# Four of six parts of the down projection as seven block products, with two weight sums of each block formed by accumulating transfers

## The chip, the cores and the metric

The kernel runs on one core of a Trainium2 chip. The metric is the device time of one execution in microseconds (us). A time that comes from a profile is that of one profiled execution, counted from the start of its span.

## The reference, cut to what matters

Two decoder layers run over 512 tokens of width 1024, all in float32. Each ends in a gated feed-forward of width 2816, and that is where the change lies:

```python
def _swiglu(h, w_gate, w_up, w_down):
    return (jax.nn.silu(h @ w_gate) * (h @ w_up)) @ w_down

for layer in range(DEPTH):
    ...
    h = h + _swiglu(_rmsnorm(h, norm_ffn[layer]), w_gate[layer], w_up[layer], w_down[layer])
return _rmsnorm(h, norm_final)
```

Layer 0 mixes tokens by stick-breaking attention, layer 1 by dilated attention with softmax; both are left alone, apart from where two of their constants are loaded.

## The kernel before, in words

Activations lie with features on the 128 partitions and the 512 tokens along the free axis. `H` holds the residual stream (8 tiles of 128x512), `X` its normalized copy, `VO` the hidden activations of the feed-forward, `R` the norm factors. Every float32 operand is split into a high part `hi` and a rest `lo`, and a product of two operands takes three matmuls: hi·hi, hi·lo, lo·hi. `Weights.split` (L268) does it for a weight tile of 128x512: a copy on ScalarE (L306), then a subtraction on VectorE (L307). The rings of split tiles are called `whi`/`wlo` and `w2hi`/`w2lo`. Raw tiles come in by DMA issued on SP (L243) into the rings `raw` (8 buffers) and `raw2` (8, in the feed-forward alone). `Weights.get` splits up to six operands ahead of the one that TensorE takes next.

The feed-forward has 22 hidden tiles of 128. The first two are done plainly. The other twenty go in ten groups g of two tiles (`product`, L981). Gate, up, and the two halves of the tokens and of the width are treated as a 2x2 block product, done by seven products P1 to P7 instead of eight, in the order of `PRODUCTS` (L46). Each product has 24 matmuls of 128x256 and takes two weight operands. Three of the operands of a block are sums of raw blocks, made on VectorE: P6 needs `s2`, the sum of three blocks (two additions, L280 and L281), P5 takes the first of these two sums, P7 needs `s3` (one addition, L287), P4 a raw block, P3 `s4` (one more addition, L291). The results are taken out of PSUM by ScalarE copies (L1003, L1012, L1015) and VectorE additions (L1005, L1016, L1018, L1025), scaled by `R` (on GpSimd for the up half, L968), passed through Silu (L963, L1009), multiplied (L971) and split into `VO` (L974 on ScalarE, L977 on VectorE).

The down projection sums over the hidden tiles in six parts (`PARTS`, L23: one of two tiles, five of four). `down` (L1036) does one of eight output tiles of one part: 12 matmuls of 128x512 for a part of four tiles, one weight operand, and one addition into `H` (L751, in `residual`). The table `BESIDE` (L48) says after which product of which group a `down` stands; with one group beside eight `down` steps of the part before, two groups and one part make a cycle. The last part stands behind all products. In layer 1 it is done by `finish` (L1052) with weights kept in `X`.

A scheduler sets the order of the instructions on every engine; each engine then runs its own list in order.

Of the kernel before, what the change touches and what calls it, by code (L numbers as in the profile page):

```python
# [7 lines left out]
F = mybir.dt.float32  # L8
# [21 lines left out]
B_RINGS = {'z': 6, 'tf': 2, 'rp': 5, 'ah': 3, 'al': 3, 'hl': 2, 'mov': 4, 'sta': 4}  # L30
# [15 lines left out]
PRODUCTS = ("P1", "P2", "P6", "P5", "P7", "P4", "P3")  # L46

BESIDE = {1: {4: (0, 3), 5: (0, 3), 6: (0, 2)}, 3: {3: (1, 1), 4: (1, 1), 5: (1, 1), 6: (1, 1)},  # L48
# [4 lines left out]


def ffn_order():

    seq = [("gu", 0), ("gu", 1)]
    done = [0] * len(PARTS)

    def out(part, count):  # L60
        for _ in range(count):
            seq.append(("dn", part, done[part]))
            done[part] += 1

    for g in range(1, NF // 2):
        for i, p in enumerate(PRODUCTS):
# [13 lines left out]
def weight_stream():  # L80
# [4 lines left out]
    def unit(key, width):  # L85
        if key not in place:
            place[key] = len(units)
            units.append((key, width))
        return place[key]

    for layer in range(2):
# [10 lines left out]
        for step in ffn_order():  # L102
# [8 lines left out]
            else:  # L111
                for i in range(2):
                    f = 2 * step[1] + i
                    w = lambda r, c: unit(("w", layer, f, r, c), 512)
                    what = {"P1": lambda: ("raw", w(0, 0)), "P2": lambda: ("raw", w(0, 1)),
                            "P6": lambda: ("s2", w(1, 0), w(1, 1), w(0, 0)), "P5": lambda: ("s1",),
                            "P7": lambda: ("s3", w(1, 0), w(0, 0)), "P4": lambda: ("raw", w(1, 1)),
                            "P3": lambda: ("s4", w(0, 1))}[step[2]]()
                    ops.append(("pr", "ffn", (*what, i) if what[0][0] == "s" else what, None))
    return units, ops  # L120


# [1040 lines left out]
```

## Time and profile before

| what | value |
|---|---|
| median of 3 runs | 1211.24 us (1210.47 to 1214.7) |
| the profiled execution | 1206.98 us, its span 1205.1 us |
| TensorE busy | 1185.0 us of the span |
| VectorE busy | 1011.8 us |
| ScalarE busy | 698.5 us |
| GpSimd busy | 173.8 us |
| granted TensorE clock, mean | 0.997 of full speed |
| both feed-forwards | from about 240 to 600 us and from about 850 us to the end |

The chain of work that ended last is followed back from the last instruction; each of its rows is a time in which nothing else could have made the end earlier. A wait in the profile names the instruction whose end released the waiting engine. Matmuls overlap, so what one costs is the distance between starts in a row of them, not its own duration.

### The profile page before, as it was taken

The page shows a single profiled execution, that of the slowest core. Times are in us where ns is not written, and L with a number is a line of the kernel's source. Part 1 is how long each engine was busy: PE and PEld are TensorE (multiplying, and loading weights), DVE is VectorE, ACT ScalarE, POOL GpSimd, SP SyncE. Part 2 cuts the span into 40 slices and gives each one's busy share as a digit, 9 for nine tenths or more (in the row PEclk, how much of TensorE's full clock was granted, in tenths as well). Part 3 has the DMA queues.
Part 4 walks back from the last instruction along what each step waited for, and adds up shares of the span by engine and source line. Part 5 has one row for each costly group of instructions (what it writes and reads, how often), then busy time and mean ns, then how long its engine had stood idle before and what let it go on. Part 6 is the DMA issues. An engine that isn't in the chain of part 4 may idle for free.

```text
span 1205.1 us, 21100 instructions
## 1 busy us (share of the span) xinstructions
PE 1185.0 (98%) x7501; PEld 1059.8 (88%) x7501; DVE 1011.8 (84%) x1831; ACT 698.5 (58%) x1331; POOL 173.8 (14%) x237
## 2 busy tenths in 40 slices
PE   9999999999999999999999999999999999999997
PEld 7989888888999999999788889887789999999996
DVE  6799999899987878787868899788899878787865
ACT  6667676685544444454466677767755444445443
POOL 0000000001100000014235443110111000000111
PEclk9999999999999999999999999999999999999998
DMA  7654644234243323332154656551343333333112
GB/s 265 177 147 113 159 114 124 62 105 140 88 125 95 115 88 114 98 106 88 36 142 132 158 136 178 133 149 53 96 141 124 113 100 102 98 113 89 45 61 70
DMA packets 74360, 138.30 MB, mean 115 GB/s; under 512 B 9616, under 2 KB 13712, under 8 KB 74256
## 3 DMA queue, kind: packets, MB, share of 16 engines
q1 hardware_dynamic: 74256, 136.97, 40.0%
q8 instruction: 59, 0.97, 0.3%
q14 instruction: 45, 0.37, 0.1%
HBM read 106.00 MB, written 2.10 MB: 90 GB/s over the span
## 4 chain that ended last, share of the span: by engine, by line
PE 87%; DVE 6%; issue 2%; DMA 2%; ACT 2%; SPq 1%; POOL 1%; POOLq 0%; DVEq 0%
PE pj L387 39%; PE z L387 30%; PE t L387 12%; PE av L387 3%; PE t L703 3%; DVE wlo L307 1%; DMA mov<-hl 1%; DMA raw<-wflat 1%; DVE w2lo L307 0%; DVE H L751 0%; SPq L243 0%; DMA H<-xg 0%; POOL H L1076 0%; DMA rp<-rp 0%; DVE sum L281 0%
## 5 line engine op out<-in xcount | busy, mean ns | idle before, releaser
L306 ACT ACTIVATE whi<-raw 128x512 fp32r<-128x512 f32 (+1 forms) x290 | 178.7, 622 | 134.5 <-PE pj L387 52.1
L307 DVE TENSOR_TENSOR wlo<-raw,whi 128x512 fp32r<-128x512 f32 (+1 forms) x290 | 206.8, 721 | 26.0 <-ACT whi L306 23.6
L387 PE MATMUL pj<-VO,whi 128*128 128x512 f32 x568 | 180.7, 398 | 1.1 <-DVE H L751 1.0
L387 PE MATMUL pj<-X,whi 128*128 128x512 f32 x480 | 154.4, 402 | 0.4
L968 POOL TENSOR_TENSOR up<-up,R 128x512 f32<-128x512 f32 x40 | 62.4, 1563 | 490.9 <-DVE up L1016 442.6
L387 PEld LDWEIGHTS pj<-VO,whi 128*128 128x128 f32 x568 | 102.4, 189 | 23.8 <-ACT whi L306 1.1
L387 PE MATMUL pj<-VO,wlo 128*128 128x512 f32 x284 | 112.7, 397 | 0.0
L751 DVE TENSOR_TENSOR H<-H,pj 128x512 f32<-128x512 f32 (+1 forms) x120 | 79.3, 664 | 32.2 <-PE pj L387 31.5
L387 PEld LDWEIGHTS pj<-X,whi 128*128 128x128 f32 x480 | 86.9, 188 | 19.1 <-ACT X L423 0.9
L387 PE MATMUL z<-XT,whi 128*128 128x256 f32 x560 | 99.7, 280 | 0.0
L306 ACT ACTIVATE w2hi<-raw 128x512 fp32r<-128x512 f32 (+1 forms) x102 | 62.8, 617 | 59.0 <-PE z L387 17.1
L387 PE MATMUL z<-X,whi 128*128 128x256 f32 (+1 forms) x464 | 96.1, 301 | 0.0
L387 PE MATMUL pj<-X,wlo 128*128 128x512 f32 x240 | 95.2, 396 | 0.5 <-DVE wlo L307 0.5
L387 PEld LDWEIGHTS z<-XT,whi 128*128 128x128 f32 x560 | 86.2, 189 | 0.7
L387 PE MATMUL pj<-VO,w2hi 128*128 128x512 f32 x264 | 83.1, 396 | 0.4 <-ACT VO L974 0.4
L307 DVE TENSOR_TENSOR w2lo<-raw,w2hi 128x512 fp32r<-128x512 f32 (+1 forms) x102 | 71.0, 698 | 12.0 <-ACT w2hi L306 11.7
L387 PEld LDWEIGHTS z<-X,whi 128*128 128x128 f32 x464 | 74.9, 189 | 4.7
L387 PE MATMUL z<-XT,wlo 128*128 128x256 f32 x280 | 78.5, 280 | 0.0
L387 PE MATMUL pj<-whi,X 128*128 128x256 f32 x384 | 74.9, 285 | 2.1 <-DVE rp L558 2.1
L387 PE MATMUL z<-XT,w2hi 128*128 128x256 f32 x400 | 74.0, 284 | 1.7 <-ACT w2hi L306 1.0
L305 POOL TENSOR_TENSOR raw<-raw,H 128x512 f32<-128x512 f32 x48 | 58.9, 1237 | 79.0 <-DMA raw<-wflat 37.1
L387 PE MATMUL z<-X,wlo 128*128 128x256 f32 (+1 forms) x232 | 69.8, 301 | 0.0
(200 smaller groups left out, 3033.0 us busy)
## 6 DMA issues: line engine op xcount, KB each, us to landing
raw<-wflat SPq DMA_DIRECT2D x384, 256.0 KB, 2.8
mov<-hl SPq DMA_DIRECT2D x64, 256.0 KB, 4.3
sta<-hl SPq DMA_DIRECT2D x64, 128.0 KB, 2.3
rp<-rp SPq DMA_DIRECT2D x56, 64.0 KB, 2.1
raw<-wflat SPq DMA_DIRECT2D x16, 128.0 KB, 2.6
H<-xg SPq DMA_DIRECT2D x7, 256.0 KB, 5.5
outT<-H SPq DMA_DIRECT2D x2, 512.0 KB, 3.0
CS<-cs SPq DMA_DIRECT2D x1, 512.0 KB, 3.7
```

The lines of the kernel that those rows point to most:

```text
L305: nc.gpsimd.tensor_mul(v3, v3, g.unsqueeze(2).to_broadcast([128, n // m, m]))
L306: nc.scalar.activation(hi[:, :n], v, AF.Copy)
L307: nc.vector.tensor_sub(lo[:, :n], v, hi[:, :n].bitcast(F))
L387: pe.matmul(out, a, b, start=start, stop=stop, skip_group_check=True)
L703: pe.transpose(b[:, o:o + 128], pr[i][:, 128 * c:128 * c + 128], idf)
L751: dve.tensor_add(H[:, n, e], H[:, n, e], p[:, e])
L968: pool.tensor_mul(two(u), two(u), r)
```

## The change

Parts 1 to 4 of the down projection, which are four hidden tiles each, are no longer done by 8 `down` steps. Each is taken as two problems q (four output tiles each), and each problem as a 2x2 block product over two pairs of hidden tiles and two halves of the tokens, done by seven products (`down_product`, steps "dq"). One has 12 matmuls of 128x256 and one weight operand, uses the banks `pj` and `av`, and ends in one VectorE addition or subtraction into a quarter of four tiles of `H` (L1154 of the new kernel). `SPREAD` and `SPREAD_LAST` place them between the products of the next two groups. Four sums of hidden blocks, needed as moving operands, are made and split by `hidden_sums`, into slot 8 of `VO`, a new tile `GS` and a free quarter of `X`; `maskB` and `ACC` serve as scratch.

The weight sums of a block are formed in another way, for gate and up (from the second group on) and for the down blocks. The block of P7 is loaded by SP and has a second block added to it by an accumulating transfer, issued on GpSimd (`Weights.add`, L278 of the new kernel). P6 then takes one VectorE addition (L326), P5 one subtraction (L330), P7 none. After P5 a second accumulating transfer adds a block to the P6 sum, which gives the operand of P3. There are 102 such transfers of 256 KB, 52 into raw tiles and 50 into sums. `raw2` shrinks to 6 buffers. P4 of the gate and up now accumulates in the bank of P1, P6 and P7, so that the addition L1016 falls away, and the sign of the token sum it takes is turned.

To make room, `CS` is loaded at the start of the second mixer and `maskB` near the end of the first feed-forward instead of before; one ring of the second mixer (`tf`) has one buffer less.

```diff
 A_RINGS = {'z': 5, 'w': 5, 'tf': 2, 'tq': 2, 'ah': 3, 'al': 3, 'hl': 2, 'mov': 4, 'sta': 4}
-B_RINGS = {'z': 6, 'tf': 2, 'rp': 5, 'ah': 3, 'al': 3, 'hl': 2, 'mov': 4, 'sta': 4}
+B_RINGS = {'z': 6, 'tf': 1, 'rp': 5, 'ah': 3, 'al': 3, 'hl': 2, 'mov': 4, 'sta': 4}
...
 PRODUCTS = ("P1", "P2", "P6", "P5", "P7", "P4", "P3")
-BESIDE = {1: {4: (0, 3), 5: (0, 3), 6: (0, 2)}, 3: {3: (1, 1), 4: (1, 1), 5: (1, 1), 6: (1, 1)},
-          4: {0: (1, 1), 2: (1, 1), 4: (1, 1), 6: (1, 1)}, 5: {3: (2, 1), 4: (2, 1), 5: (2, 1), 6: (2, 1)},
-          6: {0: (2, 1), 2: (2, 1), 4: (2, 1), 6: (2, 1)}, 7: {3: (3, 1), 4: (3, 1), 5: (3, 1), 6: (3, 1)},
...
+BLOCKED = (1, 2, 3, 4)
+BESIDE = {1: {4: 3, 6: 2}, 2: {4: 3}}
+SPREAD = ((0, 0, 1, 1, 1, 1, 1), (2, 1, 2, 1, 2, 1, 0))
+SPREAD_LAST = ((0, 0, 1, 1, 1, 1, 1), (1, 1, 1, 1, 1, 1, 0))
 def ffn_order():
     seq = [("gu", 0), ("gu", 1)]
-    done = [0] * len(PARTS)
...
+    first = 0
...
             seq.append(("pr", g, p))
-            out(*BESIDE.get(g, {}).get(i, (0, 0)))
-    for part in range(len(PARTS)):
-        out(part, 8 - done[part])
+            for _ in range(BESIDE.get(g, {}).get(i, 0)):
+                seq.append(("dn", 0, first))
+                first += 1
+            if part in BLOCKED:
+                for _ in range(spread[i]):
+                    seq.append(blocked.pop(0))
+    assert first == 8
+    seq += blocked + [("dn", len(PARTS) - 1, n) for n in range(8)]
     return seq
...
+    def block_operand(p, block, dma, ops_of):
+        w = lambda r, c: unit(block(r, c), 512)
+        low = lambda: unit(block(1, 0), 512, block(0, 0) if dma[0] else None)
+        last = () if dma[1] else (w(0, 1),)
+        what = {"P1": lambda: ("raw", w(0, 0)), "P2": lambda: ("raw", w(0, 1)),
+                "P6": lambda: ("s2", ops_of, block(0, 1) if dma[1] else None, low(), w(1, 1),
+                               *(() if dma[0] else (w(0, 0),))),
+                "P5": lambda: ("s1", ops_of, w(0, 0)), "P7": lambda: ("raw", low()),
+                "P4": lambda: ("raw", w(1, 1)), "P3": lambda: ("s4", ops_of, *last)}[p]()
+        return what
...
+                    ops.append(("pr", "ffn", block_operand(step[2], lambda r, c: ("w", layer, f, r, c),
+                                                           (step[1] > 1,) * 2, (layer, f)), None))
+            else:
+                _, part, q, p = step
+                ops.append(("dq", "ffn", block_operand(p, lambda r, c: ("d", layer, part, q, r, c),
+                                                       (True, (part, q) != (BLOCKED[-1], 1)),
+                                                       (layer, part, q)), None))
...
+            self.uring.append("raw2" if ffn and q % 14 >= 8 else "raw")
             q = q + 1 if ffn else 0
         q = 0
...
+    RAW, RAW2 = 8, 6
     W, W2 = 4, 3
...
+    def add(self, n):
+        while self.adds and self.adds[0][0] < n:
+            _, t, key = self.adds.pop(0)
+            self.nc.gpsimd.dma_start(t, self.source(key, 512), accum_op=OP.add)
     def load(self):
         u = self.nload
...
         t = self.pools[ring].tile([128, 512], F, name=ring, bufs=self.size[ring])
-        self.nc.sync.dma_start(t[:, :n], bass.AP(
...
         self.rt[u] = t[:, :n]
+        if added:
+            self.later_add(self.first[u], t, added)
...
                 self.load()
+        self.add(u + 1)
         r = [self.rt[v] for v in self.used(self.ops[u])]
         if what[0] == "raw":
             v = r[0]
         elif what[0] == "s2":
-            s1, s2 = (self.pools["sum"].tile([128, 512], F, name="sum", bufs=4) for _ in range(2))
-            nc.vector.tensor_add(s1, r[0], r[1])
-            nc.vector.tensor_add(s2, s1, r[2])
-            self.sums[what[-1]] = (s1, s2)
-            v = s2
+            v = self.pools["sum"].tile([128, 512], F, name="sum", bufs=4)
+            if len(r) == 3:
+                nc.vector.tensor_add(r[0], r[0], r[2])
+            nc.vector.tensor_add(v, r[0], r[1])
+            self.sums[what[1]] = v
         elif what[0] == "s1":
-            v = self.sums[what[-1]][0]
-        elif what[0] == "s3":
-            nc.vector.tensor_add(r[0], r[0], r[1])
             v = r[0]
+            nc.vector.tensor_sub(v, self.sums[what[1]], v)
         else:
-            v = self.sums.pop(what[-1])[1]
-            nc.vector.tensor_add(v, v, r[0])
+            v = self.sums.pop(what[1])
+            if r:
+                nc.vector.tensor_add(v, v, r[0])
         n = v.shape[1]
         ring = self.oring[u]
         if ring == "held":
-            t = self.kept[:, self.ops[u][2][1] - self.kept0]
+            t = self.kept[:, (self.ops[u][2][1] - self.kept0 + 4) % 8]
...
         nc.scalar.activation(hi[:, :n], v, AF.Copy)
         nc.vector.tensor_sub(lo[:, :n], v, hi[:, :n].bitcast(F))
+        if what[0] == "s2" and what[2]:
...
         ahead = self.AHEAD[self.ops[u][1]]
+        self.add(u + ahead + 4)
...
     ACC = sb.tile([128, 512], F, name="ACC")
-    CS = sb.tile([128, 2, 512], F, name="CS")
...
+                dve.scalar_tensor_tensor(t[0], b21, -1.0, t[1], op0=OP.mult, op1=OP.subtract)
...
+        free = X[:, 0:4, :, 256:512].rearrange("p (s c) i n -> p s i c n", s=2)
+        two = lambda t: t.rearrange("p (f n) -> p f n", f=2)
+        sums = {"P5": [two(VO[:, 8, 512 * i:512 * i + 512]) for i in range(2)],
+                "P6": [two(GS[:, i, :]) for i in range(2)],
...
-                act.activation(hi, two(g), AF.Copy)
+                if not (upper and e == 1):
+                    act.activation(hi, two(g), AF.Copy)
             def low():
-                dve.tensor_sub(lo, two(g), hi.bitcast(F))
+                if not (upper and e == 1):
...
+                high("P7", maskB)
+                low("P6", ACC)
+            def fourth():
+                b21 = st["B21"]
+                dve.scalar_tensor_tensor(b21, b21, -1.0, ACC, op0=OP.mult, op1=OP.subtract)
+                high("P4", b21)
+            for n, f in enumerate((lambda: high("P5", ACC), second, third, fourth, lambda: low("P7", maskB),
+                                   lambda: low("P4", st["B21"]))):
+                after(5 + n, f)
         def product(g, p, XT):
-            new = {"P1": ("a", zb), "P2": ("b", tb), "P5": ("e", zb), "P4": ("c", tb)}.get(p)
+            new = {"P1": ("a", zb), "P2": ("b", tb), "P5": ("e", zb)}.get(p)
             if new:
                 st[new[0]] = new[1]()
-            name = {"P1": "a", "P6": "a", "P7": "a", "P2": "b", "P5": "e", "P3": "e", "P4": "c"}[p]
-            bank = st[name]
...
                     stepped()
-            a, b, c, e = (st.get(k) for k in "abce")
...
             elif p == "P7":
-                st["u", 0], st["u", 1] = (W.pools["w2"].tile([128, 512], F, name="up", bufs=2) for _ in range(2))
+                st["u", 1] = TS()
...
+            new = {"P1": ("da", pjbank), "P2": ("db", avbank), "P5": ("de", pjbank)}.get(p)
+            if new:
+                st[new[0]] = new[1]()
+            bank = st[{"P2": "db", "P5": "de", "P3": "de"}.get(p, "da")]
+            wh, wl = W.get("dq")
+            f = PARTS[part][0]
+            def x(k, i):
+                if p in sums:
+                    return sums[p][i][:, k, :]
+                c, e = {"P1": (0, 0), "P2": (1, 0), "P3": (1, 1)}[p]
+                return VO[:, (f + 2 * c + k) % 8, 512 * i + 256 * e:512 * i + 256 * e + 256]
+            for i in range(2):
+                out = bank[:, 256 * i:256 * i + 256]
+                for k in range(2):
+                    w = slice(256 * i + 128 * k, 256 * i + 128 * k + 128)
+                    mm(out, wh[:, w], x(k, 0), bool(new) and i == 0 and k == 0, False)
+                    mm(out, wh[:, w], x(k, 1), False, False)
+                    mm(out, wl[:, w], x(k, 0), False, k == 1)
+            for r, e, op in {"P1": [(0, 0, OP.add)], "P2": [(0, 0, OP.add)], "P6": [(0, 1, OP.add)],
+                             "P5": [(1, 1, OP.subtract)], "P7": [(1, 1, OP.subtract)],
+                             "P4": [(1, 0, OP.subtract)], "P3": [(0, 1, OP.add)]}[p]:
+                h = H[:, 4 * q + 2 * r:4 * q + 2 * r + 2, 256 * e:256 * e + 256]
+                dve.tensor_tensor(h, h, two(bank), op=op)
+            stepped()
         def down(part, n):
...
                         break
                     else:
```

On TensorE, a part of four tiles took 96 matmuls of 512 columns and now takes 168 of 256 columns; the whole list grows from 7477 matmuls to 8053.

Two other engines show how instructions move. First GpSimd, in the feed-forward of layer 0 (L968 in the old and L1026 in the new kernel is the multiply of the up half by `R`; L437 and L656 before and L305 behind belong to the stages around). Before, the feed-forward is one row of its list:

```order
L656 MEMSET w 128x2
L437 TENSOR_TENSOR ACC<-H 128x512
L866 TENSOR_TENSOR s<-s,R 128x512 x2
L968 TENSOR_TENSOR up<-up,R 128x512 x18
L305 TENSOR_TENSOR raw<-raw,H 128x512 x5
```

Now, for one cycle of two groups (L278 is the issue of an accumulating transfer into a raw tile or a sum):

```order
L1026 TENSOR_TENSOR s<-s,R 128x512 x2
L278 DMA sum<-wflat 128x512 x3
L278 DMA raw_5296<-wflat 128x512
L278 DMA raw<-wflat 128x512
L278 DMA raw_5412<-wflat 128x512
L1026 TENSOR_TENSOR s<-s,R 128x512 x2
L278 DMA sum<-wflat 128x512 x2
L278 DMA raw<-wflat 128x512
L278 DMA sum<-wflat 128x512
L278 DMA raw<-wflat 128x512
L278 DMA raw_5797<-wflat 128x512
```

Twelve issues stand between four multiplies, and each waits, at the head of the list, for the load or the VectorE instruction that its tile comes from.

Second, VectorE, in the middle of the same feed-forward, with the numbers of the buffers. Before, all additions of weight blocks are its own (L280, L281, L287, L291):

```order
L291 TENSOR_TENSOR sum_5047<-sum_5047,raw_4746 128x512
L307 TENSOR_TENSOR wlo_5086<-sum_5021,whi_5085 128x512
L280 TENSOR_TENSOR sum_5355<-raw2_4966,raw2_5125 128x512
L287 TENSOR_TENSOR raw2_4966<-raw2_4966,raw2_4885 128x512
L751 TENSOR_TENSOR H_61<-H_61,pj_5089 128x512
L307 TENSOR_TENSOR wlo_5105<-sum_5046,whi_5104 128x512
L281 TENSOR_TENSOR sum_5356<-sum_5355,raw2_4885 128x512
```

Now, where a block is formed with a transfer: the first row frees the buffer into which SP then loads `raw_5273`, GpSimd's transfer adds to it, and the last row takes the sum:

```order
L350 TENSOR_TENSOR wlo_5270<-raw_4602,whi_5269 128x512
L1100 TENSOR_TENSOR g_5211<-g_5211,t_5249 128x512
L350 TENSOR_TENSOR w2lo_5291<-raw_4621,w2hi_5290 128x512
L1101 TENSOR_TENSOR g_5211<-g_5211,R_64 128x512
L1154 TENSOR_TENSOR H_61<-H_61,pj_5288 128x2x256
L350 TENSOR_TENSOR w2lo_5314<-raw2_4833,w2hi_5313 128x512
L350 TENSOR_TENSOR w2lo_5334<-raw2_4835,w2hi_5333 128x512
L350 TENSOR_TENSOR wlo_5355<-raw2_4895,whi_5354 128x512
L326 TENSOR_TENSOR sum_5578<-raw_5273,raw_5294 128x512
```

So the load and the accumulating transfer stand beside the eight VectorE instructions ahead of the last row. Of the 26 sums of that kind in a layer, five stand eight rows behind the row that frees the buffer, two stand ten rows behind, and the other nineteen 12 to 34. A whole cycle has 93 VectorE instructions in the new list and 80 in the old.

## Rows read from the trace of the kernel before

**Rows 1.** The page: busy times, GB/s in 40 slices of the span, chain that ended last.

```profile
PE 1185.0 (98%) x7501; PEld 1059.8 (88%) x7501; DVE 1011.8 (84%) x1831; ACT 698.5 (58%) x1331; POOL 173.8 (14%) x237
...
GB/s 265 177 147 113 159 114 124 62 105 140 88 125 95 115 88 114 98 106 88 36 142 132 158 136 178 133 149 53 96 141 124 113 100 102 98 113 89 45 61 70
...
PE 87%; DVE 6%; issue 2%; DMA 2%; ACT 2%; SPq 1%; POOL 1%; POOLq 0%; DVEq 0%
```

**Rows 2.** Busy time in stretches of the first feed-forward, from its third tile on.

```profile
core 0: us, PE busy (x) PEld busy (x) DVE busy (x) ACT busy (x) POOL busy (x), PEclk, DMA share, GB/s
277.00:306.00 29.00, 28.04 (x183) 24.91 (x182) 28.53 (x49) 14.84 (x28) 3.29 (x2) 1.00 0.46 146
306.00:326.00 20.00, 20.00 (x171) 20.00 (x170) 18.87 (x30) 10.73 (x18) 3.17 (x2) 1.00 0.43 132
326.00:346.00 20.00, 19.42 (x141) 18.13 (x140) 19.43 (x32) 11.22 (x20) 0.85 (x2) 1.00 0.43 125
...
406.00:466.00 60.00, 60.00 (x423) 55.85 (x422) 48.73 (x77) 28.47 (x48) 5.81 (x4) 1.00 0.36 106
```

**Rows 3.** The chain of waits, same feed-forward: start, us, engine and tile, instructions.

```profile
421.76 2.81 PE pj L387 x12
...
517.66 5.68 PE z L387 x48
...
574.66 22.69 PE pj L387 x96
```

**Rows 4.** Timeline of VectorE, first and last of sixteen instructions without a wait between.

```profile
450.08 0.69 DVE L960 TENSOR_TENSOR s<-s,R 128x512 f32<-128x512 f32 x1
...
459.10 0.69 DVE L307 TENSOR_TENSOR wlo<-raw,whi 128x512 fp32r<-128x512 f32 x1
```

**Rows 5.** Waits of VectorE, 340 to 520 us: for whom, us in total, times, longest.

```profile
DVE H L751 <- PE pj L387: 11.3, 11, 1.5
DVE s L971 <- POOL up L968: 7.1, 6, 1.2
DVE w2lo L307 <- ACT w2hi L306: 5.8, 9, 0.7
DVE wlo L307 <- ACT whi L306: 3.1, 7, 0.7
DVE VO L977 <- ACT VO L974: 2.1, 3, 0.7
```

**Rows 6.** DMA issues: KB each, median us from issue to landing.

```profile
raw<-wflat SPq DMA_DIRECT2D x384, 256.0 KB, 2.8
mov<-hl SPq DMA_DIRECT2D x64, 256.0 KB, 4.3
...
cst<-cst SPq DMA_DIRECT2D x1, 256.0 KB, 5.5
```

**Rows 7.** The multiply that GpSimd does, and the VectorE product behind it; durations in ns, least, median, most.

```profile
L968 POOL TENSOR_TENSOR up<-up,R x40: 1287/1612/2827, 288.7 to 1157.4; 128x512 f32<-128x512 f32 x40
```

**Rows 8.** ScalarE's copy after the fifth product; durations as above.

```profile
L1015 ACT ACTIVATE up<-z x20: 579/582/587, 287.2 to 1154.1; 128x512 f32<-128x512 f32 x20
```

**Rows 9.** Timeline of TensorE, end of the first feed-forward: the last part.

```profile
574.66 0.71 PE L387 MATMUL pj<-VO,w2hi 128*128 128x512 f32 x2 [0.40 <-ACT VO L974]
```

**Rows 10.** Timeline of ScalarE, same place.

```profile
573.95 0.63 ACT L974 ACTIVATE VO<-s 128x512 fp32r<-128x512 f32 x1 [0.24 <-DVE s L971]
```

More of the change, by code (lines that the diff above doesn't have):

```diff
@@ L83, in weight_stream, with unit @@
     units, ops, place = [], [], {}
[L85 to L89, printed above, removed]
+    def unit(key, width, added=None):
+        if (key, added) not in place:
+            place[key, added] = len(units)
+            units.append((key, width, added))
+        return place[key, added]
+    def block_operand(p, block, dma, ops_of):
[8 more added lines that the diff above has]
+        return what
     for layer in range(2):
@@ L110, in weight_stream @@
                             ("raw", unit(("dn", layer, *step[1:]), 128 * (b - a))), None))
-            else:
+            elif step[0] == "pr":
                 for i in range(2):
                     f = 2 * step[1] + i
[L114 to L119, printed above, removed]
+                    ops.append(("pr", "ffn", block_operand(step[2], lambda r, c: ("w", layer, f, r, c),
[5 more added lines that the diff above has]
+                                                       (layer, part, q)), None))
     return units, ops
@@ L150, in pack_weights @@
             t = cols((w_gate, w_up)[r][l], f)[:, 512 * c:512 * c + 512]
+        elif kind == "d":
+            _, _, part, q, r, c = key
+            f = 128 * (PARTS[part][0] + 2 * c)
+            t = np.concatenate([cols(w_down[l][f:f + 256], 4 * q + 2 * r + i) for i in range(2)], axis=1)
         else:
@@ L213, in __init__ @@
                 first.setdefault(u, n)
+        self.first = first
+        self.last_sum = {op[2][1]: n for n, op in enumerate(self.ops) if op[2][0] == "s4"}
         self.uring, self.oring = [], []
@@ L263, in ready @@
             return False
-        if zone == "held" and now <= self.last_product:
+        if zone == "held" and now <= self.last_product[what[1] - self.kept0 >= 4]:
             return False
@@ L760, in whole @@
                 return fs_done[1]
+            if layer:
+                CS = CSS["CS"] = rings["pool"].tile([128, 2, 512], F, name="CS")
+                sp.dma_start(CS, cs_d.rearrange("p (a n) -> p a n", a=2))
             pair = [(tb if layer else pjbank)() for _ in range(2)]
@@ L998, in product @@
                     stepped()
-            a, b, c, e = (st.get(k) for k in "abce")
+            a, b, e = (st.get(k) for k in "abe")
             f0 = 2 * g
-            if p == "P1":
-                st["g", 0] = TS()
-                act.activation(st["g", 0], a, AF.Copy)
+            if p in ("P1", "P6"):
+                h = int(p == "P6")
+                st["g", h] = W.pools["sum"].tile([128, 512], F, name="g", bufs=4)
+                act.activation(st["g", h], a, AF.Copy)
             elif p == "P2":
@@ L1115, in ffn @@
                         down(*step[1:])
+                if layer == 0:
+                    sp.dma_start(maskB, cst_d[:, 640:1152])
                 while later:
@@ L1125, in trunk @@
     W.kept = X
-    W.kept0 = next(u for u, (key, _) in enumerate(W.units) if key[:3] == ("dn", 1, len(PARTS) - 1))
+    W.kept0 = next(u for u, (key, *_) in enumerate(W.units) if key[:3] == ("dn", 1, len(PARTS) - 1))
     for c in range(8):
```

82 lines of the change are left out of this document (56 added, 26 removed), and 2 rows, old and new, of the table BESIDE.

## The prediction

> **What bounds the kernel now.** I read the page first. TensorE is busy for 1185.0 of 1205.1 us, VectorE for 84% and ScalarE for 58%, and 87% of the chain that ended last is TensorE [rows 1]. Second, the busy times by stretch of a feed-forward [rows 2]. From 406 to 466 us TensorE is busy for 60.00 of 60, at a granted clock of 1.00, and VectorE for 48.73. Third, the chain of waits [rows 3]: there it is only TensorE, one product or `down` after another. So time falls when TensorE has fewer columns to stream, as long as VectorE, the next in line, keeps up. The same rows show where it doesn't quite: from 326 to 346 us VectorE is busy for 19.43 of 20 and TensorE for 19.42.
>
> The profiled execution took 1206.98 us, 4.3 under the median of 1211.24. I work with differences and put them on the median. Some 0.5%, 6 us, is what a measurement can tell from no change.
>
> **TensorE: what is removed and added.** A `down` of 12 matmuls of 512 columns takes 2.81 us, 0.234 us each; 48 matmuls of 256 columns take 5.68 us, 0.1183 us each [rows 3]. A part had 96 × 0.234 = 22.5 us and gets 168 × 0.1183 = 19.9 us. That is −2.6 us a part, and with four parts in two layers, eight, **−20.8 us**. A cycle (two groups of seven products of 24 matmuls, and one part) was 336 × 0.1183 + 22.5 = 62.2 us and would be 59.6.
>
> A rule speaks against this. The Trainium skill ("TensorE: Matmul & The Clock Gate", Back-to-back issue gap) puts a sustained stream with weight loads at about 81 ns per matmul of 128 columns and 131 ns at 512: short matmuls pay for their weight loads. By it, 168 × at least 81 ns is 13.6 us against 96 × 131 ns = 12.6 us, an estimate in which a part gets slower. The trace disagrees, since its 512 columns take 234 ns and its 256 columns half of that, in the stream of weight loads of this very kernel.
>
> **VectorE: instructions.** In a stretch without a wait, 15 steps take 459.10 − 450.08 = 9.02 us, 0.601 us each [rows 4]. Before, a cycle has 80 instructions: 36 splits of weights, 16 additions of blocks, 8 additions into `H`, 20 for the hidden tiles. Now it has 93: 42 splits, 12 block sums, 14 into `H`, 18 for the hidden tiles (L1016 is gone), 7 for the hidden sums. So 48.1 us of 62.2 become **55.9 us of 59.6, 93.7%**. The nearest rows are the busy stretches [rows 2]: at 94.4% (306 to 326 us) TensorE lost nothing, at 97.1% (326 to 346) it lost 0.58 us in 20, 2.9%, and at 98.4% (277 to 306) 0.96 in 29, 3.3%. By these, instructions alone cost nothing yet.
>
> VectorE also waits, and in the steady stretch mostly where it had time to: 11.3 us in 180 for TensorE at L751, which is slack and shrinks. For ScalarE it waited 5.8 + 3.1 + 2.1 = 11.0 us [rows 5], 3.8 us a cycle. At 94.4% busy such waits did no harm, so I cost them at nothing; with VectorE held elsewhere they come on top. ScalarE gets about 12 more instructions of 0.6 us a cycle and had 28.47 busy of 60: no bound.
>
> **The accumulating transfers.** None is in this trace. The nearest rows [rows 6] are a plain load of the same 256 KB at 2.8 us, a copy of 256 KB that reads and writes SBUF at 4.3 us, and the slowest 256 KB at 5.5 us. Less than 2.8 us is excluded, because the same bytes come from the same memory and one more read is added. I take 4.3, since an accumulating transfer also reads what it writes. The buffer must first be loaded, so from its release to the sum of P6 it takes 2.8 + 4.3 = 7.1 us, 11.8 VectorE rows. Nineteen of the 26 sums into raw tiles in a layer have 12 rows or more. Five have 8 (4.8 us) and are 2.3 us short; two have 10 (6.0 us) and are 1.1 short: 13.7 us, less 5.7 where two stand next to each other and wait at the same time, 8 us a layer, 2.0 a cycle. The 50 sums that lead to P3 have at least 13 rows, all in time. VectorE then needs 57.9 of 59.6 us, 97.1%, at which the row loses 2.9%. The sums stand six operands ahead of TensorE, and part of a wait is eaten by that lead: I take half, 1.45% or 0.87 us a cycle, **+6.9 us** over eight. At 2.8 us the path is 5.6 us, 9.3 rows, and the cost is near 0. At 5.5 us it is 8.3 us, 13.8 rows, and the wait some 17 us a layer (second rival).
>
> The same list of GpSimd carries the multiplies L968, of 1287 to 2827 ns [rows 7]. A transfer behind one can be issued up to 2.8 us late. With four multiplies among twelve transfers I count that within the bounds above. Traffic rises from 24 to 36 transfers of 256 KB a cycle, so the 106 GB/s of the steady stretch become about 166; the first slice of the span shows 265 [rows 1], so that room is there. SP loses nothing: its loads are as many per block, and the added ones are GpSimd's.
>
> **Smaller edits.** P4 of gate and up uses the bank of P7 and so waits for ScalarE's copy, 582 ns [rows 8]. A down product of 12 × 0.118 = 1.4 us stands between and hides it; without that cover it would cost 0.6 us in each of 20 groups, 12 us at most. At the end of a feed-forward the last product is followed by work that hides the last hidden tile. The copy into `VO` ends at 574.58 [rows 10], and TensorE waited only 0.40 us for it [rows 9], after 8.4 us of cover. Now three down products (4.3 us) and the first half of two `down` (2.8) stand there, 7.1 us: up to 1.8 us lost a layer. I take **+2 us** for both, between 0 and 3.6. `CS` and `maskB`, loaded later, and the ring `tf` of one buffer, lie in stages that VectorE and TensorE share: 0, and at most a few us if a load of `CS` is awaited.
>
> **Sum:** −20.8 + 6.9 + 2 = −11.9, so 1195.1 against 1206.98 in the profiled execution, and 1211.2 − 11.9 = **1199 us** on the median.
>
> **The rivals.** *First, the whole gain.* Transfers land within 3 us, or the lead of six operands eats every wait: −20.8 + 2, about 1192. For it: at 94.4% VectorE cost TensorE nothing. Against: it stands on a plain load's price for more than a load.
>
> *Second, slower: VectorE is held at the sums of P6.* If transfers land after 5.5 us or later, its waits are 17 us a layer, 4.3 a cycle, and the waits for ScalarE (3.8) stay whole: 55.9 + 4.3 + 3.8 = 64.0 us a cycle, 1.8 over the old 62.2. Eight cycles give +14, the tail 2: about 1227. It decides from 6.3 us of waiting a cycle (62.2 − 55.9) on. For it: GpSimd's own work varies between 1.29 and 2.83 us beside a busy VectorE [rows 7], and one such delay of 1.5 us added to 4.3 gives 5.8. The Trainium skill ("SBUF — State Buffer", A bandwidth-pool intuition that's wrong) says that a transfer issued on GpSimd, some 620 ns alone, takes some 3100 ns beside a VectorE copy, because GpSimd can't write its descriptors until VectorE releases the port that they share. No row here shows such a transfer. Against it: nineteen of 26 sums have slack to spare.
>
> *Third, nothing is left.* VectorE's waits come out near those 6.3 us a cycle, and the gain of TensorE is given back: within 6 us of 1211. It needs a transfer of about 5 us.
>
> *Fourth, weight loads bound the short matmuls.* They were busy for 55.85 of 60 us with 423 matmuls, 0.132 us each [rows 2]. Were that a floor, a part would still take 168 × 0.132 = 22.2 us, 0.3 less than before, 2 us in eight; with 6.9 + 2 the time would be about 1218. Against it: 256 columns run at 0.118 [rows 3]. This is the mechanism of the Trainium skill's issue gap above.
>
> **How the numbers follow.** The forecast, a gain of 6 to 16 us, 1195 to 1205, has 0.33: its instruction counts are firm, its transfer time is not. The first rival has 0.31, because VectorE's instructions alone fit. The second has 0.21, the third 0.14, the fourth 0.01, as [rows 3] contradict it. So faster is 0.33 + 0.31 = 0.64, same 0.14, slower 0.22. The range begins at 1189, the whole gain without a loss at the tail, and ends at 1226, short of the far half of the second rival: 0.05 below and 0.13 above are left out.
>
> **What would show it.** In the new profile, down products should run at 0.118 us a matmul, and TensorE's idle time in the steady stretches should be 0.5 to 1.5 us a cycle, released by VectorE's splits or by its additions into `H`. VectorE should be above 90% busy there, its longest waits at L326, released by transfers into raw tiles. Transfers should land in 3.5 to 5 us. If they land under 3, the first rival holds; if the idle time before L326 exceeds 6 us a cycle, the second or third. Wrong altogether would be a matmul pitch over 0.13 us, a lower granted clock, or a wait at a place not named here, such as GpSimd's multiply held up behind transfers that wait for loads.

## The result, and the profile after

The changed kernel takes **1271.23 us** (median of 4 runs, 1267.61 to 1273.11) against 1210.86 of the kernel before in the same series: a ratio of 1.0489, 95% interval 1.0456 to 1.0521. It is 60 us slower. 1199 us was forecast, and the range ended at 1226.

The page of the changed kernel has these lines on busy time, on the chain that ended last and on DMA issues (columns as in [rows 1] and [rows 6]):

```profile
PE 1187.2 (94%) x8077; PEld 1089.5 (86%) x8077; DVE 1082.7 (86%) x1925; ACT 740.0 (58%) x1423; POOL 255.2 (20%) x339
...
PE 41%; DVE 16%; DMA 10%; issue 5%; ACT 2%; POOL 1%; DVEq 0%; POOLq 0%; SPq 0%; ACTq 0%
...
raw<-wflat SPq DMA_DIRECT2D x384, 256.0 KB, 3.1
mov<-hl SPq DMA_DIRECT2D x64, 256.0 KB, 4.5
raw<-wflat POOLq DMA_DIRECT2D x52, 256.0 KB, 4.9
sum<-wflat POOLq DMA_DIRECT2D x50, 256.0 KB, 5.6
```

TensorE has 41% of the chain, DMA 10% and VectorE 16%. These shares can't be set beside the 87% of before as they stand: the new chain can be followed back only to 312 us, so they add up to about 75%. Of what it covers TensorE has a little over half. The accumulating transfers are the two rows on POOL's queue: 4.9 us into raw tiles, 5.6 into sums. The steady part of the first feed-forward, in three stretches of about one cycle each (columns as in [rows 2]):

```profile
330.00:400.00 70.00, 64.23 (x536) 63.35 (x535) 60.54 (x95) 35.24 (x62) 16.90 (x18) 1.00 0.60 136
400.00:470.00 70.00, 62.77 (x490) 61.96 (x489) 59.67 (x94) 34.62 (x61) 15.91 (x17) 0.93 0.58 136
470.00:540.00 70.00, 64.59 (x521) 63.98 (x520) 60.88 (x96) 36.29 (x64) 17.71 (x19) 0.95 0.61 138
```

TensorE, busy without a gap before, now idles 5.4 to 7.2 us in 70, and its granted clock is 0.93 and 0.95 on the mean of the last two stretches. VectorE isn't full either: 9 to 10 us of each stretch are not busy. Its waits, 340 to 520 us (for whom, us in total, times, longest), and those of TensorE:

```profile
DVE sum L326 <- DMA raw<-wflat: 19.4, 4, 8.4
DVE sum L326 <- DVE w2lo L350: 0.6, 1, 0.6
DVE sum L326 <- DVE wlo L350: 0.4, 1, 0.4
```

```profile
PE pj L433 <- DVE H L1154: 10.4, 5, 3.7
PE pj L433 <- ACT g L1021: 2.1, 2, 1.4
PE z L433 <- ACT g L1098: 1.9, 1, 1.9
```

Nearly all waiting of VectorE is at L326, the sum of P6, for a transfer into a raw tile; a fifth such wait, of 7.8 us, ends at 520.80 and is not in these rows. The waits of [rows 5], 11.3 us for TensorE and 11.0 for ScalarE, are gone: VectorE runs behind everyone, and TensorE waits for its additions into `H`. No wait of VectorE in these rows is for TensorE, so the slower clock can have cost these cycles little. That it cost nothing isn't shown, since the chain also passes through TensorE at half the clock. There 12 matmuls of 256 columns take 2.90 us, and 1.42 us a little later:

```profile
458.10 2.90 PE pj L433 x12
...
464.69 1.42 PE pj L433 x12
```

The chain shows one path through a transfer in full:

```profile
380.40 0.61 DVE wlo L350
381.01 0.02 issue
381.03 2.52 DMA raw<-wflat
383.55 0.02 issue
383.57 0.04 POOLq L278
383.62 0.49 issue
384.11 5.65 DMA raw<-wflat
389.76 0.04 DVEq L326
389.80 0.04 issue
389.84 0.09 DVE sum L326
```

The split at 380.40 frees a raw buffer. SP's load lands 2.5 us later, GpSimd needs 0.56 us to see it and issue, the accumulating transfer takes 5.65 us, and at 389.84 VectorE may add: **8.8 us**, 14.7 rows of 0.601 us, where I had taken 7.1.

A second thing shows in the lists of GpSimd and VectorE (start, duration):

```profile
391.82 2.97 POOL L1026 TENSOR_TENSOR s<-s,R 128x512 f32<-128x512 f32 x2 [6.85 <-DVE s L1107]
```

```profile
391.65 0.68 DVE L1154 TENSOR_TENSOR H<-H,pj 128x512 f32<-128x512 f32 x1
392.25 1.40 DVE L350 TENSOR_TENSOR wlo<-raw,whi 128x512 fp32r<-128x512 f32 x1
393.57 0.68 DVE L1154 TENSOR_TENSOR H<-H,pj 128x512 f32<-128x512 f32 x1
394.16 1.18 DVE L350 TENSOR_TENSOR wlo<-raw,whi 128x512 fp32r<-128x512 f32 x1
```

Beside GpSimd's two multiplies, two subtractions of VectorE on SBUF tiles take 1.40 and 1.18 us instead of 0.68, and each holds up the next. The addition between them, which reads PSUM, is not stretched.

To compare kernels I use the time of three cycles of layer 0 (from the third to the ninth Silu of the first half, L1009 before, L1103 now; layer 1 agrees within 2.4 us): 335.36 to 521.19 us is 185.8 before, 339.37 to 547.82 is 208.4 now. With 206.4 in layer 1, these six cycles hold 43 of the 60 us; the rest lies ahead of them and behind them in the feed-forwards.

### The profile page after: what moved, and what is told of

It is laid out like the page before. It is cut to its first block, busy times and chain, and to the rows that moved or that the text cites. A ratio compares the mean times of both kernels' runs of the same rounds, so it can differ in the third digit from the quotient of the medians.

```text
span 1265.8 us, 22739 instructions
## 1 busy us (share of the span) xinstructions
PE 1187.2 (94%) x8077; PEld 1089.5 (86%) x8077; DVE 1082.7 (86%) x1925; ACT 740.0 (58%) x1423; POOL 255.2 (20%) x339
## 4 chain that ended last, share of the span: by engine, by line
PE 41%; DVE 16%; DMA 10%; issue 5%; ACT 2%; POOL 1%; DVEq 0%; POOLq 0%; SPq 0%; ACTq 0%
PE pj L433 17%; PE z L433 16%; DMA raw<-wflat 9%; DVE wlo L350 5%; PE t L433 4%; DVE w2lo L350 2%; PE av L433 2%; DVE H L1154 2%; PE t L749 1%; DMA mov<-hl 1%; DVE raw L330 1%; DVE g L1034 1%; DVE g L1018 1%; DVE g L1117 1%; ACT whi L349 0%
## 5 line engine op out<-in xcount | busy, mean ns | idle before, releaser
L349 ACT ACTIVATE whi<-raw 128x512 fp32r<-128x512 f32 x331 | 201.2, 619 | 151.9 <-PE pj L433 91.4
L350 DVE TENSOR_TENSOR wlo<-raw,whi 128x512 fp32r<-128x512 f32 x331 | 241.8, 735 | 15.2 <-ACT whi L349 14.2
L433 PE MATMUL pj<-X,whi 128*128 128x512 f32 (+1 forms) x592 | 178.2, 385 | 24.8 <-DVE H L1154 13.2
L433 PE MATMUL pj<-VO,whi 128*128 128x512 f32 (+1 forms) x544 | 142.0, 350 | 15.6 <-DVE H L797 7.8
L433 PE MATMUL z<-XT,w2hi 128*128 128x256 f32 x656 | 125.0, 290 | 8.0 <-ACT g L1098 6.7
L433 PEld LDWEIGHTS z<-XT,w2hi 128*128 128x128 f32 x656 | 105.4, 197 | 10.3 <-ACT g L1098 7.8
L433 PE MATMUL pj<-X,wlo 128*128 128x512 f32 (+1 forms) x296 | 112.0, 378 | 0.2 <-DVE wlo L350 0.2
L433 PE MATMUL z<-XT,w2lo 128*128 128x256 f32 x328 | 94.4, 289 | 1.2 <-DVE w2lo L350 1.0
L278 POOL DMA_DIRECT2D raw<-wflat x52 | 45.1, 879 | 245.4 <-DMA raw<-wflat 73.7
L433 PE MATMUL pj<-VO,wlo 128*128 128x256 f32 (+1 forms) x272 | 94.2, 346 | 0.0
L1026 POOL TENSOR_TENSOR s<-s,R 128x512 f32<-128x512 f32 x40 | 58.0, 1472 | 99.1 <-DVE s L1107 70.9
L326 DVE TENSOR_TENSOR sum<-raw 128x512 f32<-128x512 f32 x36 | 29.3, 814 | 55.3 <-DMA raw<-wflat 53.8
```

Of the source, the lines that this page charges most:

```text
L278: self.nc.gpsimd.dma_start(t, self.source(key, 512), accum_op=OP.add)
L326: nc.vector.tensor_add(v, r[0], r[1])
L349: nc.scalar.activation(hi[:, :n], v, AF.Copy)
L350: nc.vector.tensor_sub(lo[:, :n], v, hi[:, :n].bitcast(F))
L433: pe.matmul(out, a, b, start=start, stop=stop, skip_group_check=True)
L1026: pool.tensor_mul(two(u), two(u), r)
```

## The experiments

The theory: VectorE is the bound, and transfers that land too late hold it at L326. Rivals: the list of VectorE alone is too long, or short matmuls and a falling clock of TensorE cost it. All ratios are to the kernel before on the same chip.

**No transfers.**

```diff
-            self.nc.gpsimd.dma_start(t, self.source(key, 512), accum_op=OP.add)
+            pass
```

> The accumulating transfers are left out, so the weight sums lack the block that each would have added; loads, VectorE's additions and all products stay, and the scheduler orders the lists anew. Theory (VectorE is held at the sums of P6 by transfers that land too late): the 68.5 us of waiting at L326 go, a cycle falls from 69 to between 59.6 and 61 us, and the time to 1192 to 1204 us, as the whole gain was forecast. First rival (VectorE's instruction list alone is the new bound, 93 rows at 0.64 us): a cycle of at least 60 us and the waits at L326 replaced by others, 1204 to 1215 us. Second rival (short matmuls or the clock of TensorE cost it): over 1230 us.

Measured: 1200.69 us, 0.9911 (0.9887 to 0.9935). Three cycles take 183.1 us, 61.0 each. Busy times from 340 to 520 us, and the only wait of VectorE:

```profile
340.00:520.00 180.00, 177.49 (x1488) 176.26 (x1488) 177.74 (x276) 103.95 (x182) 16.55 (x12) 1.00 0.36 105
```

```profile
DVE sum L326 <- DMA raw<-wflat: 1.8, 5, 0.5
```

So the transfers cost 1271.2 − 1200.7 = **70.5 us**; this includes what the new order of the lists does. In the changed kernel, the waits for transfers at L326 come to nearly as much over the whole run (us in total, times):

```profile
  DVE sum L326: 68.5, 16
```

The theory holds for them, and the time lies in its range. But what the first rival named shows in the rest: VectorE is now full (177.74 of 180), at 177.74 / 276 = 0.644 us an instruction instead of 0.601, and a cycle takes 61.0 us, not 59.6.

**Plain transfers.** Same lists, no addition in the transfer.

```diff
-            self.nc.gpsimd.dma_start(t, self.source(key, 512), accum_op=OP.add)
+            self.nc.gpsimd.dma_start(t, self.source(key, 512))
```

> The 102 transfers on GpSimd are plain loads into the same tiles instead of accumulating ones, so the sums are replaced by the second block; all lists stay the same. Theory, in the form that the read before the write makes them late: they land in 2.8 to 3.3 us instead of 4.9, the path from a freed buffer to the sum falls from 9 to about 7 us, the waits at L326 to under half of 68.5 us, and the time to 1215 to 1235 us. Rival (issue on GpSimd and its list in order make them late, the addition costs little): they land in over 4.4 us and the time stays over 1255 us.

Measured: 1230.92 us, 1.016 (1.0133 to 1.0188). The theory holds. The landing times, VectorE's largest wait from 340 to 520 us, and the waits for transfers at L326 in the whole run:

```profile
raw<-wflat POOLq DMA_DIRECT2D x52, 256.0 KB, 3.2
sum<-wflat POOLq DMA_DIRECT2D x50, 256.0 KB, 3.1
```

```profile
DVE sum L326 <- DMA raw<-wflat: 13.6, 4, 3.9
```

```profile
  DVE sum L326: 33.0, 14
```

The addition costs 1.7 us a transfer into a raw tile and 2.5 into a sum, and 40 of the 70 us. The other 30 go with the 33.0 us of waits that are left, for a second transfer behind the first: 2.8 + 0.6 + 3.2 us is still more than the 4.8 us that five of the sums of a layer have.

The median landing hides two cases. Of the 102 accumulating transfers of the changed kernel, 43 were issued with no other one under way and landed in a median of 4.2 us, 59 with another under way and landed in 5.8. Plain ones took 3.0 and 3.2 us. Of the transfers into sums 35 of 50 are of the second kind, of those into raw tiles 24 of 52. Whether one transfer holds up the other wasn't tried by itself.

**All sums on VectorE; then only those into raw tiles.**

```diff
-                                                           (step[1] > 1,) * 2, (layer, f)), None))
+                                                           (False, False), (layer, f)), None))
...
-                                                       (True, (part, q) != (BLOCKED[-1], 1)),
+                                                       (False, False),
```

In the second kernel the two new lines are:

```diff
+                                                           (False, step[1] > 1), (layer, f)), None))
...
+                                                       (False, (part, q) != (BLOCKED[-1], 1)),
```

> All weight sums on VectorE, no transfers: 12 more VectorE instructions a cycle, 105 of 0.601 to 0.641 us, 63.1 to 67.3 us a cycle against 62.2 before and 69 with the transfers. Theory (VectorE is the bound, the transfers hold it): no wait at L326, 1215 to 1250 us, faster than the change. Rival (TensorE's short matmuls or its clock cost it, VectorE has room): no better than 1262 us.

> Only the 52 transfers into raw tiles are taken back, as additions on VectorE; the 50 into P6 sums stay: 99 VectorE instructions a cycle, 59.5 to 63.5 us. Theory (it is the transfers into raw tiles, with a load before them and a full ring, that hold VectorE; those into sums have time): waits for transfers under 10 us in all and 1198 to 1228 us, the best of these versions that compute everything. Rival (any transfer in GpSimd's list holds VectorE): waits for sums appear in their place and the time is over 1245 us.

Measured: 1248.53 us, 1.0309 (1.0287 to 1.0331), and 1237.01 us, 1.0213 (1.0176 to 1.0249). The first kernel's busy times from 340 to 520 us:

```profile
340.00:520.00 180.00, 169.34 (x1393) 165.59 (x1393) 179.75 (x283) 93.45 (x164) 21.66 (x12) 1.00 0.33 100
```

Here VectorE is busy for 179.75 of 180 with no transfer and no wait: its list is the bound, 105 × 0.635 = 66.7 us a cycle, and 66.0 were measured. That the change is still 23 us slower than this says that a transfer costs VectorE more by waiting than the addition that it saves. The second kernel missed its range by 9 us: 99 rows at 0.637 make 63.1, and its waits didn't vanish (VectorE, 340 to 520 us):

```profile
DVE raw L325 <- DMA raw<-wflat: 5.7, 3, 2.4
DVE sum L326 <- DMA raw<-wflat: 1.6, 1, 1.6
```

These are for plain loads on SP. Why loads come late here and not in the kernel without any transfer wasn't tried.

**An earlier load, and the multiply on VectorE.**

```diff
-                "P2": lambda: ("raw", w(0, 1)),
+                "P2": lambda: (low(), ("raw", w(0, 1)))[1],
```

```diff
-                pool.tensor_mul(two(u), two(u), r)
+                dve.tensor_mul(two(u), two(u), r)
```

> The change, with the block of P7 (the one that a transfer adds to) loaded ahead of that of P2 instead of behind it, one or two loads earlier. Theory (the path from the freed buffer to the sum of P6, 9 us with load, issue and landing, is longer than its lead): the lead grows by one to two loads of 2.9 us each, the waits at L326 fall from 68.5 us to 20 to 45, and the time to 1225 to 1255 us. Rival (14 raw buffers that are held longer set the pace, whatever the order): within 8 us of 1271, with waits moved to other loads.

> The change, with the multiply of the up half (L1026, four a cycle) on VectorE instead of GpSimd. Theory (VectorE is the bound, and its rows beside a GpSimd multiply are stretched, by 3.5 to 4.1 us a cycle): four more rows of 0.602 us are 2.4, and 3.5 to 4 us go, so a cycle gains 1.1 to 1.6 and the time falls by 9 to 13 us, to 1258 to 1263. Rival (the stretch comes from the issue of transfers on GpSimd): the stretch stays and the time grows by some 19 us.

Measured: 1226.82 us, 1.0145 (1.012 to 1.017), 44 us better than the change, with 27.2 us of waits for transfers at L326 instead of 68.5, as the theory has it. The order of two loads gives back as much as the addition in the transfer cost, as a path too long for its lead would have it, and a ring of too few buffers would not. The multiply gives 1246.31 us, 1.03 (1.0281 to 1.0319), 25 us better where 9 to 13 were expected. Busy times and the largest wait of VectorE, 340 to 520 us, with the multiply moved:

```profile
340.00:520.00 180.00, 169.54 (x1386) 168.40 (x1385) 160.05 (x265) 93.90 (x166) 28.67 (x33) 0.97 0.63 148
```

```profile
DVE wlo L350 <- ACT whi L349: 14.6, 3, 6.7
```

160.05 / 265 = 0.604 us an instruction: the stretch is gone, so it was the multiplies' and not the transfers'. The waits for transfers at L326 are gone from this stretch too, but others took their place, at splits behind ScalarE. A cycle fell by 4.1 us, and the instructions explain 0.8 of it: 97 × 0.604 = 58.6 us instead of 93 × 0.639 = 59.4. The rest is waiting that went, which the expectation didn't have. The multiplies no longer stand between the transfers in GpSimd's list; that this is why is not shown.

**Both repairs.** Both edits above.

> The change with both repairs: the block of P7 loaded earlier and the multiply on VectorE. VectorE has 97 rows a cycle, 58.4 us without stretch, TensorE 59.6. The waits were 9.5 to 11 us a cycle, 5 to 6 with the earlier load, 6 to 8 with the multiply. Theory (the two repairs add up): 2 to 4 us of waiting are left, 60.4 to 62.4 us a cycle, 1197 to 1214 us. Rival (transfers in one list, 12 a cycle of some 5 us from issue to landing, hold VectorE whatever is done): 4 us of waiting or more, over 1214 us.

Measured: 1218.8 us, 1.0074 (1.0057 to 1.009): the rival. Waits of VectorE, then of ScalarE, 340 to 520 us:

```profile
DVE wlo L350 <- ACT whi L349: 13.0, 3, 7.0
```

```profile
ACT whi L349 <- DMA sum<-wflat: 15.7, 3, 8.0
```

ScalarE's copy of the P3 operand waits for the transfer into the sum, up to 8.0 us, and VectorE behind it. The longest of these waits, with the two rows of GpSimd's list ahead of it (start, duration, idle before):

```profile
429.26 0.86 POOL L278 DMA_DIRECT2D raw<-wflat  x1 [5.27 <-DVE w2lo L350]
429.80 1.22 POOL L278 DMA_DIRECT2D sum<-wflat  x1
437.11 0.63 ACT L349 ACTIVATE whi<-sum 128x512 fp32r<-128x512 f32 x1 [7.97 <-DMA sum<-wflat]
```

The transfer into the sum shows no wait of its own. It is issued at 429.80, right behind one into a raw tile that had waited 5.27 us for a split of VectorE, and takes 7.2 us to land. It is one of the 50 that I had costed at nothing.

**No transfers, and the multiply on VectorE.**

> The change without its transfers (the sums lack the block that each would have added) and with the multiply of the up half on VectorE: 97 VectorE rows a cycle, 58.4 us, against TensorE's 59.6. Theory (the term of TensorE was right, and VectorE alone stood in its way): TensorE is the bound again, 59.6 to 60.1 us a cycle, 1187 to 1195 us. Rival (short products lose something of their own): cycles of 60.6 us or more and no better than the 1200.7 us of the version without transfers.

Measured: 1190.24 us, 0.9837 (0.982 to 0.9853), a cycle of 59.6 us, and TensorE never waits from 340 to 520 us:

```profile
340.00:520.00 180.00, 180.00 (x1523) 180.00 (x1522) 177.97 (x295) 108.15 (x187) 0.00 (x0) 1.00 0.37 109
```

The term of TensorE was right: 504 matmuls of 256 columns at 0.1183 us are 59.6. And VectorE at 98.9% busy took nothing from it.

**Half of the block products, no transfers; then also the multiply on VectorE.** One problem of a part is done by products, the other four output tiles by `down`; both flags are (False, False) as above, the hidden quarter that `down` needs is split too, and the second kernel has the edit of the multiply.

```diff
-            blocked = [("dq", part, q, p) for q in range(2) for p in DOWN_PRODUCTS]
+            blocked = [("dq", part, 1, p) for p in DOWN_PRODUCTS] + [("dn", part, n) for n in range(4)]
...
-SPREAD = ((0, 0, 1, 1, 1, 1, 1), (2, 1, 2, 1, 2, 1, 0))
+SPREAD = ((0, 0, 1, 1, 1, 1, 1), (1, 1, 1, 1, 1, 1, 0))
...
-SPREAD_LAST = ((0, 0, 1, 1, 1, 1, 1), (1, 1, 1, 1, 1, 1, 0))
+SPREAD_LAST = ((0, 0, 1, 1, 1, 1, 1), (1, 1, 1, 0, 0, 0, 0))
```

> Only one of the two problems of a part is done by block products, the other four output tiles by down steps as before, and all weight sums on VectorE, no transfers. TensorE's cycle is 39.76 + 7 x 1.42 + 4 x 2.81 = 60.9 us against 62.2; VectorE has 96 rows a cycle, 57.8 us, and 3.6 of stretch, 61.4. Theory (a cycle is the larger of TensorE's time and VectorE's rows at 0.602 us with the stretch): 61.2 to 62 us a cycle, 1202 to 1211 us. Rival (the short products themselves cost more than their columns): over 1215 us.

> As the half-blocked version, with the multiply of the up half on VectorE: 100 rows a cycle, 60.2 us without the stretch, against 60.9 of TensorE. Theory: 60.9 to 61.5 us a cycle, 1200 to 1207 us, a little faster than the half-blocked version and than the kernel before. Rival (the stretch has another cause): 100 rows and 3.6 us, 63.8 us a cycle, about 1223 us.

Measured: 1219.31 us, 1.0069 (1.0053 to 1.0084), and **1200.63 us, 0.9922 (0.9908 to 0.9936)**. The first missed by 8 us: a cycle takes 62.7 us, more than either engine needs. Its time is in the rival's range, but short products that cost more than their columns are excluded by the second, which has the same matmuls. The busy times of both, 340 to 520 us:

```profile
340.00:520.00 180.00, 175.11 (x1333) 167.59 (x1332) 176.40 (x278) 94.71 (x167) 20.16 (x12) 1.00 0.33 102
```

```profile
340.00:520.00 180.00, 179.09 (x1367) 171.45 (x1366) 178.99 (x297) 100.84 (x174) 0.00 (x0) 1.00 0.33 105
```

In the first, neither TensorE nor VectorE is full. The largest wait of TensorE and the longest of VectorE, 340 to 520 us:

```profile
PE z L433 <- ACT s L1104: 4.0, 3, 1.7
```

```profile
DVE g L1034 <- POOL s L1026: 1.2, 1, 1.2
```

TensorE waits for a copy of ScalarE out of PSUM. That copy stands in ScalarE's list behind splits of sums, which wait for VectorE. The last of the three times, in ScalarE's timeline (start, duration, idle before):

```profile
471.55 0.63 ACT L349 ACTIVATE w2hi<-sum 128x512 fp32r<-128x512 f32 x1 [3.22 <-DVE sum L334]
...
472.61 0.58 ACT L1104 ACTIVATE s<-z 128x512 f32<-128x512 f32 x1
```

So a VectorE that is late holds TensorE through ScalarE's list. In the second VectorE does 19 more instructions in the same 180 us, 0.603 us each, and a cycle is 61.0 us, TensorE's own 60.9. This version beats the kernel before by 10 us, and the change by 70.

**Control: the kernel before, with the multiply on VectorE.**

> The kernel before with the multiply of the up half on VectorE, and nothing else. Theory (before, TensorE is the bound, with 11 us of slack on VectorE a cycle): within 4 us of 1211. Rival (the half-blocked version owes its gain to the multiply and not to fewer columns): 1204 us or less.

Measured: 1205.54 us, 0.996 (0.9947 to 0.9973). Neither holds: some 4.4 us of the ten come from the multiply alone, the rest from what else the half-blocked version changes, fewer columns above all. In the steady stretch TensorE is busy throughout before and after. Of the 2.9 us between the two profiles, 1.3 lie in the full stretches of [rows 2], 277 to 346 us, where TensorE idled 1.5 us and now idles 0.25; where the rest lies isn't shown. Two of these stretches now read

```profile
277.00:306.00 29.00, 28.75 (x191) 25.97 (x190) 28.85 (x52) 15.31 (x30) 0.00 (x0) 1.00 0.44 146
...
326.00:346.00 20.00, 20.00 (x148) 18.92 (x147) 19.97 (x34) 10.32 (x19) 0.00 (x0) 1.00 0.52 160
```

with TensorE busy for 28.75 instead of 28.04 us, and for 20.00 instead of 19.42.

All versions in one view (instructions of VectorE a cycle by the lists; busy time by instructions, 340 to 520 us; a cycle is a third of the three in layer 0). A dash stands where VectorE waits so often between instructions that busy time by instructions doesn't tell a row's step:

| version | VectorE instr. a cycle | us each | a cycle, us | median, us |
|---|---|---|---|---|
| before | 80 | – | 61.9 | 1210.9 |
| the change | 93 | 0.639 | 69.5 | 1271.2 |
| plain transfers | 93 | 0.641 | 64.8 | 1230.9 |
| no transfers | 93 | 0.644 | 61.0 | 1200.7 |
| all sums on VectorE | 105 | 0.635 | 66.0 | 1248.5 |
| raw sums on VectorE | 99 | 0.637 | 65.4 | 1237.0 |
| earlier load | 93 | 0.638 | 64.7 | 1226.8 |
| multiply on VectorE | 97 | 0.604 | 65.4 | 1246.3 |
| earlier load and multiply | 97 | 0.602 | 63.9 | 1218.8 |
| no transfers, multiply | 97 | 0.603 | 59.6 | 1190.2 |
| half | 96 | 0.635 | 62.7 | 1219.3 |
| half, multiply | 100 | 0.603 | 61.0 | 1200.6 |
| before, multiply | 84 | – | 61.6 | 1205.5 |

## Why the prediction was wrong

With the versions above the 60 us come apart into three terms: −19.4 us from TensorE's columns (no transfers, multiply moved), +9 from VectorE's stretched instructions (no transfers), +70.5 from the transfers.

**TensorE's −20.8 us** was right. With VectorE out of the way a cycle takes 59.6 us, as worked out. By the issue gap of the Trainium skill ("TensorE: Matmul & The Clock Gate", Back-to-back issue gap) a part would have got slower; the 59.6 us of that run, as [rows 3] before it, contradict the rule.

**VectorE's instructions at nothing** failed. I took 0.601 us from a stretch of [rows 4] without a multiply of GpSimd in it. A cycle has four, and 93 instructions take 0.639 to 0.644 us each, 59.4 to 59.9 us instead of 55.9. This fills the cycle of 59.6 us, with no transfer at all, and a gain of 10 us is left where 19 were possible. The 1.29 to 2.83 us of [rows 7] were in view: I read them as GpSimd's trouble beside VectorE, and not as VectorE's beside GpSimd. The kernel before could hardly show the price: of its 12 multiplies from 340 to 520 us, three lengthened a VectorE instruction, by 0.6 us in all, since beside them VectorE mostly waited or added from PSUM. In the version without transfers all 12 did, by 11.0 us. The step from a busy share to a loss of TensorE failed with it: TensorE lost nothing beside a VectorE busy for 98.9%, once the multiplies were gone from GpSimd. The Trainium skill ("SBUF — State Buffer", Who interferes with whom) says that a VectorE instruction with two SBUF inputs contends with a GpSimd instruction that reads SBUF. The trace agrees: 1.40 and 1.18 us for subtractions of two SBUF tiles beside the multiplies, 0.68 for the addition from PSUM between.

**The transfers at +6.9 us** is the step that failed most: they cost 70.5. The number of late sums was nearly right, 14 of 52 counted and 16 measured. Their waits were not: 4.3 us each on the mean, where 2.3 was the most that was counted. The price of 4.3 us a transfer holds for those issued with no other under way (4.2); the medians of all, 4.9 and 5.6, lie near the bound of 5.5. Three parts of the working were wrong beyond the price. First, the 0.6 us between the load's landing and the issue was left out, so the path above was 8.8 us. Second, I took half of each wait as eaten by the lead of six operands. But a lead is eaten once, and with VectorE full it doesn't come back. The totals fit this: 68.5 us of waits at L326 and 70.5 us lost. Third, I counted buffer rows of each tile by itself, as if each transfer could start once its own load had landed. All twelve of a cycle and the multiplies stand in one list, and what waits at its head holds those behind it, as at 429 us in the version with both repairs. So the 50 transfers into sums, with at least 13 rows each, cost too: with both repairs, ScalarE still waited 15.7 us in 180 for them.

**The second rival** had the place and the sign: VectorE held at the sums of P6. Its 1227 us was 44 low: it had 55.9 us of instructions instead of 59.4, and 4.3 us a cycle of waits for transfers, where 69.5 − 59.4 = 10.1 us are left for all waits. The 3.8 us of waits for ScalarE that it kept did vanish. Against it I had put the slack of nineteen sums; that slack assumed a list without other work. The delay of issuing beside VectorE, which it had as an argument, doesn't show: plain transfers issued on GpSimd landed in 3.2 and 3.1 us, with VectorE busy for 165 of 180 us.

**The tail at +2 us** was too small for the change: TensorE waits 4.7 us for ScalarE at the end of the first feed-forward, against 0.40 before, and 2.1 us without transfers and with the multiply on VectorE. At the end of the second no such wait shows. The smaller edits cost nothing where VectorE keeps up: in that last kernel TensorE waits for nothing from 340 to 520 us.

The chances, 0.22 for slower, followed from these sums. They took VectorE to have 3.7 us a cycle of room (59.6 − 55.9), when 59.4 to 59.9 us of instructions left none for any wait. The lower granted clock, which the prediction named as a sign of being wrong altogether, came with TensorE's waits; by how much it adds to them wasn't measured by itself.

## What to carry to other kernels

Where a change takes time from the bound and gives work to the next engine, cost the second engine's instructions from a stretch that holds everything that will run beside them, and count every wait whole once it is full. An accumulating transfer is not a free addition: it puts load, issue and transfer in a row, and its tile's lead must cover all three and what stands ahead of it in the issuing list. When the second engine has only part of the room, do part of the change: half of the block products, with every sum on VectorE and the multiply moved there, fitted and gained 10 us; all of them, with their sums, did not fit in any version that was tried.

## What the runs showed of the hardware

- An accumulating transfer of 256 KB into SBUF, issued on GpSimd, landed in a median of 4.9 us (raw tiles) and 5.6 us (sums), a plain one on the same queue in 3.2 and 3.1, a load on SP in 2.8 in the kernel before and 3.1 in the changed one. With no other accumulating transfer under way it took 4.2 us, with one 5.8.
- A multiply on GpSimd beside a full VectorE cost VectorE about 0.9 us: (0.639 − 0.601) × 93 is 3.5 us a cycle, for four, and without transfers 12 multiplies cost it 11.0 us. On VectorE the same multiply costs 0.60 us. Moved there, the kernel was faster in all five pairs that were run, by 4 to 25 us.
- In the changed kernel TensorE's granted clock fell to half, 1.2 GHz, for 3 to 7 us at a time behind waits of TensorE (means of 0.93 and 0.95 in the stretches above). From 456 to 463 us, behind a wait of 3.7 us, 12 matmuls of 256 columns took 2.90 us instead of 1.42. What it cost the kernel wasn't measured by itself.
